# Trunk kernel: V split before the normalising products, k prepared before q, and K's other half written by ScalarE and GpSimd

## The chip, the cores and the metric

The kernel runs on one core of a Trainium2 chip. The metric is the device time of one execution in microseconds (us), the median of several runs. The core has five engines that each work through a list of instructions of their own and wait for one another with semaphores: TensorE (PE in the profile) multiplies matrices and transposes, VectorE (DVE) and ScalarE (ACT) do element-wise work and can read PSUM, the memory into which TensorE writes, GpSimd (POOL) does element-wise work on SBUF, and SyncE (SP) issues the transfers (DMAs).

## The reference

A decoder trunk of two layers on x of shape (1, 512, 1024) in float32. Each layer is an RMS norm, an attention mixer with a residual, another RMS norm, and an MLP with a squared ReLU, 1024 to 4096 and back, with a residual.

- Layer 0: one input projection gives 8 heads A (dilated sliding windows with ALiBi) and 8 heads B (a window of 128, two shared k/v heads, learned sinks). The head size is 64.
- Layer 1: 16 heads C with a causal mask and a forget gate, whose cumulated logs are added to the scores.

In all heads q and k are normalised per head before the scores:

```python
aq = rms_norm(aq.reshape(bsz, seq, N_HEADS_A, HEAD_DIM), a_q_gain)
ak = rms_norm(ak.reshape(bsz, seq, N_HEADS_A, HEAD_DIM), a_k_gain)
s = jnp.einsum("bqhd,bqjhd->bhqj", qb, kg).astype(jnp.float32) * scale
p = jnp.exp(s - m)
num = jnp.einsum("bhqj,bqjhd->bhqd", p.astype(v.dtype), vg)
```

## The kernel before

**Numbers as pairs.** TensorE multiplies rounded operands (float32r). Each operand is therefore held as a rounded part and a remainder, high and low, and a product takes three matmuls: high by high, low by high, high by low. Weights arrive by DMA in `wraw` tiles and are split into `whi` and `wlo`; a pattern names the engines that write the two. Activations are split in the same manner, by `scale_split` (L158) where they are scaled too: ScalarE writes the high part, DVE the remainder.

**Layer 0's beginning.** `start` (L613) loads x and the first weights, multiplies for q and k of the first four heads A into four PSUM banks of the pool pA, and builds the distance tables in between. It then calls `norm_heads` (L243): ScalarE copies the banks to `qk` tiles (L250) and squares them (L254), DVE sums the squares per head (L255), and `rsqrt_small` (L120) takes the inverse roots in a chain of small DVE operations (L130 to L135). Since the norm of the whole token enters too, its inverse root is taken in the same chain; the squares' and the roots' scratch lies in one buffer named `sq`. The loop at L271 multiplies q and k by the roots for each of the four blocks of 128 tokens, the first and third on DVE and the others on GpSimd (`NORM`), and L276 copies the token's root to `rcol`.

Then `v_a(0)` multiplies for V into four pA banks. Its `prep_v` (L310) needs `rcol` and splits each bank, which gives the banks back for `kv_b` (k and v of the heads B), and `kv_b` runs as dense work beside the first attention heads.

**Attention.** `run` (L446) interleaves steps of attention (scores, softmax, transposes of P, values) with dense projections, in a fixed proportion, in the program's text. For each pair of heads `get` calls `prep_q` (L286) and then `prep_k` (L297). Each transposes a 128-column block of `qk` on TensorE into a pB bank (`head_T`, L279) and splits it. Q has for each head one half with the high part and the other half with the remainder over the 128 partitions. K has for each head a tile in which `k[:, 0]` is the high part and `k[:, 1]` the remainder, each of them in both halves of the partitions: `scale_split` fills the half in which the head's transpose lies, and a DMA on SyncE's queue (L306) copies both parts to the other half. There are 13 such pairs, 26 K tiles: 4 pairs of heads A, one for the heads B, 8 of heads C.

**What sets the order.** A planner goes over the program with estimated times and orders each engine's list; an instruction that is earlier in the text goes first where both are ready. `in_order` (L144) fixes an instruction behind the one before it on its engine in the text, while `cnt["start"]` holds. In the attention stages nothing is fixed; in the MLP nearly everything is. Tiles with one `tag` share a number of buffers, `bufs`, and a new one waits until an old one is done with. P3 is the tag of the tables' scratch and of the widest P tile.

Of the kernel before, what the change touches and what calls it, by code (L numbers as in the profile page):

```python
# [9 lines left out]
F32 = mybir.dt.float32  # L10
# [59 lines left out]
def trunk(ctx, tc, x, b_sinks, w_out_even, b_forget, w_out_odd, w_up, w_down, xt, gains, w_in_even, w_in_odd, out):  # L70
# [10 lines left out]
    def bank(tag, name):  # L81
        return ps.tile([P, 512], F32, tag=tag, bufs=BANKS[tag], name=name)
# [61 lines left out]
    def in_order(m):  # L144
        if cnt["start"]:
            tc.keep_in_program_order(m)
# [50 lines left out]
    def layer_attention(li, hT, w_in, w_out, stats=None):  # L197


        with ExitStack() as c2:  # L200
# [42 lines left out]
            def norm_heads(outs, nh, sq_tag="sq", sq_bufs=1 + li, ms=None):  # L243


                w = nh * HD
                qk = [ap.tile([P, 2, 512], F32, tag="qk", bufs=4, name="qk") for _ in range(2)]
                ss = small.tile([P, NT, 8], F32, tag="ss", name="ss")
                for t in range(NT):
                    nc.scalar.copy(qk[t // 2][:, t % 2, :w], outs[t][:, :w])  # L250
                for t in range(NT):
                    q = qk[t // 2][:, t % 2, :w]
                    sq = ap.tile([P, 512], F32, tag=sq_tag, bufs=sq_bufs, name="sq")
                    nc.scalar.activation(sq[:, :w], q, AF.Square)  # L254
                    nc.vector.reduce_sum(ss[:, t, :nh], sq[:, :w].rearrange("p (h d) -> p h d", d=HD), axis=AX.X)  # L255
                if ms is None:
                    v = small.tile([P, NT, 8], F32, tag="ssv", name="ssv")[:, :, :nh]
                    rs = small.tile([P, NT, 8], F32, tag="rs", name="rs")[:, :, :nh]
                    room = None
                else:  # L260
                    room = ap.tile([P, 512], F32, tag=sq_tag, bufs=sq_bufs, name="room")
                    room = [room[:, i * NT * (nh + 1):(i + 1) * NT * (nh + 1)]
                            .rearrange("p (t h) -> p t h", h=nh + 1) for i in range(5)]
                    v, rs = room[:2]
                    nc.vector.tensor_scalar(v[:, :, nh], ms, 1.0 / D, EPS, op0=OP.mult, op1=OP.add)
                    nc.vector.tensor_scalar_mul(ecol, v[:, :, nh], EPS)
                for t in range(NT):
                    nc.vector.tensor_scalar(v[:, t, :nh], ss[:, t, :nh], 1.0 / HD, ecol[:, t:t + 1],
                                            op0=OP.mult, op1=OP.add)
                rsqrt_small(rs, v, room)  # L270
                for t in range(NT):  # L271
                    q = qk[t // 2][:, t % 2, :w].rearrange("p (h d) -> p h d", d=HD)
                    eng = nc.gpsimd if NORM[t] == "g" else nc.vector
                    eng.tensor_mul(q, q, rs[:, t, :nh].unsqueeze(2).to_broadcast([P, nh, HD]))
                if ms is not None:
                    nc.vector.tensor_copy(rcol, rs[:, :, nh])  # L276
                return qk

            def head_T(qk, off):  # L279
# [6 lines left out]
            def prep_q(qk, off):  # L286

                pt = head_T(qk, off)
                q = ap.tile([P, 2, 512], F32R, tag="Q", bufs=2, name="Q")
                for h in range(2):  # L290
                    r = slice(h * HD, (h + 1) * HD)
                    r2 = slice((1 - h) * HD, (2 - h) * HD)
                    nc.scalar.copy(q[r, h], pt[r])
                    nc.vector.tensor_sub(q[r2, h], pt[r], q[r, h].bitcast(F32))
                return q

            def prep_k(qk, off, g):  # L297

                pt = head_T(qk, off)
                ks = []  # L300
                for h in range(2):
                    k = ap.tile([P, 2, 512], F32R, tag="K", bufs=3, name="K")
                    r = slice(h * HD, (h + 1) * HD)
                    r2 = slice((1 - h) * HD, (2 - h) * HD)
                    scale_split(k[r, 0], k[r, 1], pt[r], g[r])
                    nc.sync.dma_start(k[r2].bitcast(F32), k[r].bitcast(F32))  # L306
                    ks.append(k)
                return ks

            def prep_v(outs, off, nh, i):  # L310

                V = vset[i % 2]
                for t in range(NT):
                    src = outs[t][:, off:off + nh * HD].rearrange("p (h d) -> p h d", d=HD)
                    scale_split(V[:, t, :nh, :HD], V[:, t, :nh, HD:], src, rcol[:, t:t + 1])
                return V
# [193 lines left out]

            def v_use(g, i):
                def use(outs):
                    st["v", g] = prep_v(outs, 0, 4, i)
                return use

            def qk_use(key, nh, *sq):
                def use(outs, ms=None):
                    st["qk", key] = norm_heads(outs, nh, *sq, ms=ms)
                return use
# [5 lines left out]
            if li == 0:  # L525
                def qk_a(g):
                    return project([(g * 768, g * 768 + 512)], qk_use(g, 8))

                def v_a(g):
                    return project([(g * 768 + 512, g * 768 + 768)], v_use(g, 0), PAT_START if g == 0 else PAT_ATT)  # L530

                def att_a(g):
                    def get(p_):
                        qk = st["qk", g]
                        return prep_q(qk, p_ * P), prep_k(qk, 256 + p_ * P, gg[:, 0:1])
                    return attend(get, 256, lambda: st["v", g], lambda j: j, "a", 4 * g, 2, 2 * g)

                def kv_b():
                    def use(outs):
                        st["v", 3] = prep_v(outs, P, 2, 1)  # L540
                        st["k", "b"] = norm_heads(outs, 2)
                    return project([(2048, 2304)], use, PAT_START)

                def att_b():
                    def get(p_):
                        if p_ == 0:
                            st["kb"] = prep_k(st["k", "b"], 0, gg[:, 1:2])
                        k = st["kb"][p_ // 2]
                        return prep_q(st["qk", "b"], p_ * P), [k, k]
                    return attend(get, 0, lambda: st["v", 3], lambda j: j // 4, "b", 0, 4, 4)  # L550

                start(ap, hT, w_in, make_tables(ap, dist, lt, lb), [bank("pA", f"pj{t}") for t in range(NT)], qk_use(0, 8))
                all_of(v_a(0))
                run(att_a(0), 32, chain(kv_b(), project([(1536, 2048)], qk_use("b", 8))), 768, LEADS[0])
                run(att_b(), NB, chain(qk_a(1), v_a(1)), 768, LEADS[1])
                run(chain(att_a(1), last_values()), 38, chain(out_part([0, 1, 4, 5], True),
                                                              out_part([6, 7], False), ahead([2, 3])), 1536, LEADS[2])
                last = [2, 3]
            else:
                def qk_c(g):  # L560
                    return project([(g * 768, g * 768 + 512)], qk_use(g, 8))

                def v_c(g):
                    return project([(g * 768 + 512, g * 768 + 768)], v_use(g, g))

                def vf_c():
                    def use(outs):
                        forget(ap, outs)
                        v_use(0, 0)(outs)
                    return project([(512, 768), (3072, 3088)], use, PAT_START)  # L570

                def att_c(g):
                    def get(p_):
                        qk = st["qk", g]
                        return prep_q(qk, p_ * P), prep_k(qk, 256 + p_ * P, gg[:, 2:3])
                    return attend(get, 256, lambda: st["v", g], lambda j: j, "c", 4 * g, 2, 2 * g)

                g = vf_c()
                for _ in range(STATS):
                    next(g)  # L580
                stats()
                all_of(g)
                all_of(qk_c(0))
                for g in range(3):
                    run(att_c(g), 36, chain(qk_c(g + 1), v_c(g + 1)), 768, LEADS[3 + g])
                run(chain(att_c(3), last_values()), 42, chain(out_part([0, 1, 2, 3], True),
                                                              out_part([4, 5], False), ahead([6, 7])), 1536, LEADS[6])
                last = [6, 7]
# [683 lines left out]
```

## Time and profile before

| | |
|---|---|
| runs, median (lowest to highest) | 1165.46 us (1165.13 to 1166.15) |
| the profiled execution: its time | 1166.66 us |
| its span in the trace | 1164.9 us |
| mean granted TensorE clock | 0.997 |
| PE busy | 1145.0 us, 98% |
| DVE busy | 875.5 us, 75% |
| ACT busy | 645.9 us, 55% |
| POOL busy | 200.3 us, 17% |

The attention of layer 0 lies from about 45 to 240 us of the span, its MLP from there to about 570, the attention of layer 1 from there to about 830, and its MLP behind that. A row of the timeline has the start in us, the duration in us, engine, line, operation, what it writes and reads, its shape and how many are merged; in brackets the idle time of the engine before it and what ended that. A row of waits has the engine that waited, its line, what it waited for, and then the sum in us, the number of waits and the longest. In tables of windows each engine's busy time is followed by the granted TensorE clock, the busy share of the DMA engines and GB/s.

### The profile page before, as it was taken

To read this page: it belongs to the slowest core of one execution; us is meant where nothing else is said; L and a number is where in the kernel's file an instruction comes from. 1 tells how busy PE (TensorE), PEld (TensorE's weight loads), DVE (VectorE), ACT (ScalarE), POOL (GpSimd) and SP (SyncE) were. 2 spreads that over 40 slices of the span, in tenths; PEclk is the share of its full clock that TensorE was granted. 3 is DMA by queue.
4 is the path that set the end of the run, shared out by engine and by line. 5 is a ranking of instruction groups with operands and counts; after the bars stand their busy time and mean duration, and the time that the engine had idled before them with its cause. 6 is when DMAs were issued, how large, how long until landed. Compare 5 with 4: busy or idle time off the path is not lost.

```text
span 1164.9 us, 17364 instructions
## 1 busy us (share of the span) xinstructions
PE 1145.0 (98%) x6228; PEld 980.3 (84%) x6228; DVE 875.5 (75%) x1865; ACT 645.9 (55%) x1342; POOL 200.3 (17%) x292
## 2 busy tenths in 40 slices
PE   9899999999999999999999999999999999999998
PEld 7887887888988988988887888888888888888887
DVE  7787899968967847855646877778858759669676
ACT  7365867565545545444335685656756455465452
POOL 0345434200000000000155445342100000000000
PEclk9899999999999999999999999999999999999999
DMA  8423115242332332333443333343430721623403
GB/s 287 129 75 91 37 37 148 71 127 73 102 116 91 91 109 91 93 118 106 149 122 121 106 86 109 95 133 112 164 104 4 234 90 56 197 73 109 148 34 109
DMA packets 94695, 126.57 MB, mean 109 GB/s; under 512 B 5888, under 2 KB 66304, under 8 KB 94608
## 3 DMA queue, kind: packets, MB, share of 16 engines
q1 hardware_dynamic: 93568, 123.29, 34.7%
q10 hardware_dynamic: 1040, 2.16, 0.5%
q8 instruction: 49, 0.80, 0.3%
q14 instruction: 38, 0.31, 0.1%
HBM read 114.39 MB, written 4.23 MB: 102 GB/s over the span
## 4 chain that ended last, share of the span: by engine, by line
PE 84%; DVE 7%; DMA 3%; ACT 3%; issue 2%; POOL 2%; SPq 0%; POOLq 0%; ACTq 0%; DVEq 0%
PE up L165 10%; PE up L168 10%; PE up L169 10%; PE pj L236 4%; PE pj L234 4%; PE pj L235 4%; PE O L398 3%; PE PT L378 2%; PE op L169 2%; PE op L165 2%; PE op L168 2%; PE Y L1032 2%; PE Y L1030 2%; PE Y L1033 2%; PE S L341 2%
## 5 line engine op out<-in xcount | busy, mean ns | idle before, releaser
L165 PE MATMUL up<-xin,whi 128*128 128x512 f32 x512 | 200.5, 392 | 0.0
L169 PE MATMUL up<-xin,whi 128*128 128x512 f32 x512 | 199.3, 389 | 0.0
L168 PE MATMUL up<-xin,wlo 128*128 128x512 f32 x512 | 199.2, 389 | 0.0
L779 ACT CAST whi<-wraw 128x512 fp32r<-128x512 f32 x228 | 139.2, 619 | 105.1 <-PE up L169 47.4
L780 DVE TENSOR_TENSOR wlo<-wraw,whi 128x512 fp32r<-128x512 f32 x228 | 151.6, 685 | 50.9 <-ACT whi L779 50.8
L169 PEld LDWEIGHTS up<-xin,whi 128*128 128x128 f32 x512 | 96.1, 188 | 20.2
L165 PEld LDWEIGHTS up<-xin,whi 128*128 128x128 f32 x512 | 96.1, 188 | 19.8 <-issue 0.2
L168 PEld LDWEIGHTS up<-xin,wlo 128*128 128x128 f32 x512 | 96.2, 188 | 19.6 <-issue 0.2
L358 ACT ACTIVATE P<-P,negm 128x128 f32<-128x128 f32 (+5 forms) x128 | 69.4, 543 | 46.5 <-DVE negm L355 44.6
L153 POOL TENSOR_SCALAR whi<-wraw 128x512 fp32r<-128x512 f32 x88 | 60.1, 684 | 167.3 <-PE pj L236 123.6
L961 ACT ACTIVATE u<-up 128x512 f32<-128x512 f32 x64 | 38.3, 599 | 90.9 <-PE up L169 90.9
L234 PE MATMUL pj<-whi,hn 128*128 128x512 f32 (+2 forms) x256 | 88.7, 347 | 0.0
L236 PE MATMUL pj<-whi,hn 128*128 128x512 f32 (+2 forms) x256 | 86.9, 340 | 0.0
L235 PE MATMUL pj<-wlo,hn 128*128 128x512 f32 (+2 forms) x256 | 86.8, 339 | 0.0
L800 DVE TENSOR_TENSOR t<-u 128x256 f32<-128x256 f32 x56 | 23.1, 423 | 62.9 <-ACT u L1104 61.1
L156 POOL TENSOR_TENSOR wlo<-wraw,whi 128x512 fp32r<-128x512 f32 x48 | 64.0, 1335 | 21.0 <-ACT whi L151 18.6
L366 POOL TENSOR_SCALAR P<-P,rden 128x256 f32<-128x256 f32 (+2 forms) x96 | 48.9, 512 | 81.5 <-DVE rden L361 76.0
L156 DVE TENSOR_TENSOR wlo<-wraw,whi 128x512 fp32r<-128x512 f32 (+1 forms) x71 | 48.2, 685 | 18.5 <-POOL whi L153 15.0
L390 ACT CAST PT<-PT 128x256 fp32r<-128x256 f32 (+3 forms) x128 | 49.1, 403 | 21.5 <-PE PT L378 20.6
L234 PE MATMUL pj<-whi,h 128*128 128x256 f32 (+1 forms) x160 | 55.4, 346 | 4.6 <-DVE v L161 4.1
L355 DVE CUSTOM_DVE_ANT_0 P<-S,bias 128x128 f32<-128x128 f32 (+1 forms) x96 | 45.7, 485 | 17.8 <-PE S L344 11.9
L779 ACT CAST whi<-mraw 128x512 fp32r<-128x512 f32 x64 | 38.8, 619 | 33.1 <-DVE mraw L890 14.4
(241 smaller groups left out, 3092.1 us busy)
## 6 DMA issues: line engine op xcount, KB each, us to landing
wraw<-in_w_up SPq DMA_DIRECT2D x64, 512.0 KB, 4.3
wraw<-in_w_down SPq DMA_DIRECT2D x56, 512.0 KB, 3.8
wraw<-in_w_in_odd SPq DMA_DIRECT2D x22, 512.0 KB, 3.8
wraw<-in_w_in_even SPq DMA_DIRECT2D x17, 512.0 KB, 4.7
mraw<-in_w_down SPq DMA_DIRECT2D x16, 512.0 KB, 4.7
K<-K SPq DMA_DIRECT2D x26, 256.0 KB, 2.9
bias<-csp SPq DMA_DIRECT2D x16, 256.0 KB, 3.3
wraw<-in_w_out_odd SPq DMA_DIRECT2D x8, 512.0 KB, 3.8
```

Of the source, the lines that this page charges most:

```text
L153: nc.gpsimd.tensor_scalar(dst_h, src, 1.0, 1.0, op0=OP.mult, op1=OP.mult)
L156: in_order((nc.gpsimd if lo == "pool" else nc.vector).tensor_sub(dst_l, src, dst_h.bitcast(F32)))
L165: m = nc.tensor.matmul(o, wh, xh, start=start, stop=False, skip_group_check=more)
L168: nc.tensor.matmul(o, wl, xh, start=False, stop=False, skip_group_check=more)
L169: nc.tensor.matmul(o, wh, xl, start=False, stop=stop, skip_group_check=more)
L234: nc.tensor.matmul(o, xh, hi[:, :n], start=k == 0, stop=False)
L235: nc.tensor.matmul(o, xh, lo[:, :n], start=False, stop=False)
L236: nc.tensor.matmul(o, xl, hi[:, :n], start=False, stop=k == DC - 1)
L358: nc.scalar.activation(p[:, :ne], p[:, :ne], AF.Exp, scale=-1.0, bias=negm[:, i:i + 1], accum_out=den[:, i:i + 1])
L390: nc.scalar.copy(dst[:, 0], pt[:, :n])
L779: sca(nc.scalar.copy(dst_h, src))
L780: late.append(lambda: vec(nc.vector.tensor_sub(dst_l, src, dst_h.bitcast(F32))))
```

## The change

- `norm_heads` puts the products with the inverse roots into a function, `normalise`. At the start (where the token's norm comes along) it isn't called at once but stored; `v_use`, after V has been split, calls it. V's split and DVE's products are fixed in this order.
- The squares of this first call lie in two buffers with the tag P3, not in one with the tag `sq`.
- `get` of the heads A and C calls `prep_k` before `prep_q`.
- In `prep_k` the DMA is gone. ScalarE writes the high part of the other half from PSUM with a second activation, and GpSimd copies the remainder.

```diff
@@ norm_heads
-                for t in range(NT):
-                    q = qk[t // 2][:, t % 2, :w].rearrange("p (h d) -> p h d", d=HD)
-                    eng = nc.gpsimd if NORM[t] == "g" else nc.vector
-                    eng.tensor_mul(q, q, rs[:, t, :nh].unsqueeze(2).to_broadcast([P, nh, HD]))
-                if ms is not None:
+                def normalise():
+                    for t in range(NT):
+                        q = qk[t // 2][:, t % 2, :w].rearrange("p (h d) -> p h d", d=HD)
+                        eng = nc.gpsimd if NORM[t] == "g" else nc.vector
+                        m = eng.tensor_mul(q, q, rs[:, t, :nh].unsqueeze(2).to_broadcast([P, nh, HD]))
+                        if eng is nc.vector:
+                            in_order(m)
+
+                if ms is None:
+                    normalise()
+                else:
                     nc.vector.tensor_copy(rcol, rs[:, :, nh])
+                    st["first"] = normalise
                 return qk
@@ prep_k
                     scale_split(k[r, 0], k[r, 1], pt[r], g[r])
-                    nc.sync.dma_start(k[r2].bitcast(F32), k[r].bitcast(F32))
+                    nc.scalar.activation(k[r2, 0], pt[r], AF.Copy, scale=g[r])
+                    nc.gpsimd.tensor_copy(k[r2, 1], k[r, 1].bitcast(F32))
@@ v_use
                 def use(outs):
+                    first = st.pop("first", None)
+                    cnt["start"] = first is not None
                     st["v", g] = prep_v(outs, 0, 4, i)
+                    if first:
+                        first()
+                    cnt["start"] = False
                 return use
@@ att_a; att_c in the same manner
-                        return prep_q(qk, p_ * P), prep_k(qk, 256 + p_ * P, gg[:, 0:1])
+                        k = prep_k(qk, 256 + p_ * P, gg[:, 0:1])
+                        return prep_q(qk, p_ * P), k
@@ layer 0
-                start(ap, hT, w_in, make_tables(ap, dist, lt, lb), [bank("pA", f"pj{t}") for t in range(NT)], qk_use(0, 8))
+                start(ap, hT, w_in, make_tables(ap, dist, lt, lb), [bank("pA", f"pj{t}") for t in range(NT)], qk_use(0, 8, "P3", 2))
```

More of the change, by code (lines that the diff above doesn't have):

```diff
@@ L574, in get @@
                         qk = st["qk", g]
-                        return prep_q(qk, p_ * P), prep_k(qk, 256 + p_ * P, gg[:, 2:3])
+                        k = prep_k(qk, 256 + p_ * P, gg[:, 2:3])
+                        return prep_q(qk, p_ * P), k
                     return attend(get, 256, lambda: st["v", g], lambda j: j, "c", 4 * g, 2, 2 * g)
```

## The prediction

> **What bounds the kernel now.** I read the page first, then who waited for whom, then the windows around the largest wait, then the engines one by one in that stretch. The page:
>
> ```profile
> span 1164.9 us, 17364 instructions
> PE 1145.0 (98%) x6228; PEld 980.3 (84%) x6228; DVE 875.5 (75%) x1865; ACT 645.9 (55%) x1342; POOL 200.3 (17%) x292
> PE 84%; DVE 7%; DMA 3%; ACT 3%; issue 2%; POOL 2%; SPq 0%; POOLq 0%; ACTq 0%; DVEq 0%
> ```
>
> TensorE (PE) is busy 98% of the span and carries 84% of the chain that ended last. The change removes no matmul, so it can only win back time in which PE stands still or runs slowly. PE's waits, with the total, the count and the longest in us:
>
> ```profile
> PE pj L234 <- DVE v L161: 4.1, 2, 3.5
> ...
> PE S L341 <- DMA K<-K: 1.9, 3, 1.1
> PE S L341 <- DVE yf L402: 1.3, 1, 1.3
> PE PT L378 <- DVE negm L355: 1.1, 1, 1.1
> PE qkT L283 <- POOL qk L274: 1.0, 2, 0.5
> ```
>
> The largest is the first: kv_b's matmuls wait for a pj bank until V has been read out of it. The second is the transfer that fills K's other half. PE's list shows where the first lies:
>
> ```profile
> 41.35 0.28 PE L235 MATMUL pj<-wlo,h 128*128 128x256 f32 x1
> 41.47 0.28 PE L236 MATMUL pj<-whi,h 128*128 128x256 f32 x1
> 45.25 0.39 PE L234 MATMUL pj<-whi,h 128*128 128x256 f32 x1 [3.50 <-DVE v L161]
> ```
>
> PE ends v_a(0) at 41.75 and stands until 45.25, 3.50 us; of the 4.1 us in two waits 0.6 are left for the second, for the fourth V tile. (Matmuls of this form start 0.12 us apart: 41.35, 41.47.) The windows (from and to, the width, the busy us of PE, of its weight loads, of DVE, ACT and POOL, then the granted clock) show a second cost:
>
> ```profile
> 42.00:44.00 2.00, 0.00 (x0) 0.00 (x0) 2.00 (x2) 0.00 (x0) 2.00 (x2) 1.00 0.00 0
> ...
> 46.00:48.00 2.00, 1.38 (x8) 0.99 (x7) 1.57 (x2) 0.00 (x0) 0.63 (x1) 0.59 0.00 0
> 48.00:50.00 2.00, 2.00 (x11) 2.00 (x11) 0.08 (x1) 0.58 (x1) 0.00 (x0) 0.50 0.71 223
> 50.00:52.00 2.00, 2.00 (x11) 2.00 (x11) 1.69 (x3) 1.61 (x3) 0.00 (x0) 0.50 0.10 39
> 52.00:54.00 2.00, 2.00 (x15) 2.00 (x14) 0.91 (x2) 0.34 (x1) 0.62 (x1) 0.70 0.61 131
> ...
> 160.00:200.00 40.00, 36.80 (x208) 30.93 (x207) 37.59 (x99) 26.21 (x69) 17.46 (x22) 1.00 0.40 114
> ```
>
> After the standstill the granted clock is 0.59, 0.50, 0.50 and 0.70 in four windows of 2 us, with PE busy nearly all the time: 2 x (0.41 + 0.50 + 0.50 + 0.30) = 3.4 us of matmul time lost. So this place costs 3.50 + 0.6 + 3.4 = 7.5 us.
>
> **Part 1: V before the products with the norms.** Why V comes late is on DVE's list, with ScalarE's and GpSimd's rows beneath it:
>
> ```profile
> 40.81 0.20 DVE L135 SCALAR_TENSOR_TENSOR room<-room 128x36 f32<-128x36 f32 x1
> 41.04 2.14 DVE L274 TENSOR_TENSOR qk<-qk,room 128x512 f32<-128x512 f32 x2
> 43.11 1.00 DVE L276 COPY rcol<-room 128x4 f32<-128x4 f32 x1
> 44.71 1.27 DVE L161 SCALAR_TENSOR_TENSOR v<-pj,rcol,v 128x256 fp32r<-128x256 f32 x3 [0.60 <-ACT v L160]
> 45.90 1.28 DVE L156 TENSOR_TENSOR wlo<-wraw,whi 128x512 fp32r<-128x512 f32 x1
> ```
> ```profile
> 44.21 1.57 ACT L160 ACTIVATE v<-pj,rcol 128x256 fp32r<-128x256 f32 x4 [9.05 <-DVE rcol L276]
> ```
> ```profile
> 41.14 2.95 POOL L274 TENSOR_TENSOR qk<-qk,room 128x512 f32<-128x512 f32 x2 [3.07 <-issue]
> ```
>
> The inverse roots are done at 41.01. Two products (2.14) and the copy of rcol (1.00) stand before V, and ScalarE has been idle 9.05 us for rcol. Moved behind V, these products cost V nothing. rcol then follows the roots at once: 0.17 us by a 128x4 operation alone (quoted below), 1.00 by its own row beside GpSimd's products. I take 0.2, because GpSimd started 0.1 us after DVE in the row above.
>
> **Part 2: squares with two buffers, under P3's name.** ScalarE's squares wait for DVE's reductions, one buffer between them (ScalarE's waits from 28 to 40; its last cast of V's and kv_b's weights; a small DVE operation alone):
>
> ```profile
> ACT sq L254 <- DVE ss L255: 1.2, 3, 0.7
> ```
> ```profile
> 33.67 0.60 ACT L151 CAST whi<-wraw 128x512 fp32r<-128x512 f32 x1
> ```
> ```profile
> 35.91 0.17 DVE L265 TENSOR_SCALAR room<-ms 128x4 f32<-128x4 f32 x1
> ```
>
> The three waits sum to 1.2 us. The gain is between 0 (if the tables' scratch, which has the same name, still holds a buffer) and 1.2; I take 1.2, since those tables are finished before the squares begin. Roots end at 39.8, rcol at 40.0. ScalarE's V tiles start 0.1 later at 0.39 each (1.57 for four), DVE's 0.5 behind them: the first bank is free near 41.1, before PE ends at 41.75. The fourth tile's matmuls end only at 41.75, so it is through near 42.8; PE asks for it after three triples of 3 x 0.12 = 0.36, at 42.8. PE's idle time left here: I take 0.3, between 0 and 1.9 (no gain from the buffers, and the full 1.00 for rcol). **Parts 1 and 2: 3.50 + 0.6 - 0.3 = 3.8, and the clock's 3.4, together 7.2 us.** What is late next is qk: its two DVE products end near 42.8 + 2.14 = 44.9 instead of 43.18. Cover is kv_b: 32 triples at 0.36 are 11.5 us of matmuls that need only V's banks. The last cast of its weights, at 33.67 above, is done by 34.3. Without that cover the whole 3.2 us would be idle again (a rival below).
>
> **Part 3: K's other half by ScalarE and GpSimd.** K's rows (min/median/max ns), and its transfer's landing:
>
> ```profile
> L160 ACT ACTIVATE K<-qkT,gg x26: 682/684/689, 50.2 to 789.6; 64x512 fp32r<-64x512 f32 x26
> L161 DVE SCALAR_TENSOR_TENSOR K<-qkT,gg,K x26: 735/750/757, 50.9 to 790.4; 64x512 fp32r<-64x512 f32 x26
> L306 SPq DMA_DIRECT2D K<-K x26: 461/467/522, 51.7 to 791.2; - x26
> ...
>   ACT K L160: 4.0, 12
> ...
> DMA to landing us min/median/max: 2.8/2.9/4.9
> ```
> ```profile
> L156 POOL TENSOR_TENSOR wlo<-wraw,whi 128x512 fp32r<-128x512 f32 x48 | 64.0, 1335 | 21.0 <-ACT whi L151 18.6
> L153 POOL TENSOR_SCALAR whi<-wraw 128x512 fp32r<-128x512 f32 x88 | 60.1, 684 | 167.3 <-PE pj L236 123.6 <-DVE room L265 22.8 <-issue 7.4
> L366 POOL TENSOR_SCALAR P<-P,rden 128x256 f32<-128x256 f32 x40 | 22.1, 554 | 10.8 <-DVE rden L361 10.4
> ```
>
> Removed: 26 issues on SP and 2.9 us from issue to landing after each DVE part. SP's queue only becomes freer: a weight load no longer stands behind an issue that waits for K. Added: 26 ScalarE activations of the same form as L160, 0.684 each, 17.8 us; and 26 GpSimd copies of 64x512, which no row shows: 0.554 by the 128x256 row, 1.335 by the two-input row. I take 0.684, the row with one input and 512 columns: 17.8 us. After DVE's part K is complete in about 0.7 us, not 2.9, so the 1.9 us of PE's wait for K go: **gain 1.9** (0 to 1.9). k ahead of q delays Q by at most the four K activations, 2.7 us, but S needs both, and K with its transfer was the later one.
>
> What the additions cost others: ScalarE is 3% of the chain, 35 us of its 646 busy, so 5.4% of what it does sets the end: 17.8 x 0.054 = 1.0. GpSimd by the same sum: 23 of 200.3 are 12%, 2.1; I take 0.8, because the copy stands where the transfer's wait was. **Cost 1.8 us**, between 0 and 17.8 (all of ScalarE's addition on the path). DVE may also be slowed by GpSimd's copies: the product with two SBUF inputs at 45.90 took 1.28 beside GpSimd, but K's own L161, which reads PSUM, keeps to 735-757 throughout. I take nothing.
>
> [...]
>
> **Sum.** 7.2 + 1.9 - 1.8 = 7.3 us. The profiled execution took 1166.66 us, 1.76 more than its span; the runs shown have a median of 1165.46, 1.2 below it. 1166.66 - 7.3 = 1159.4 profiled, 1158.2 as a median. The instructions of the attention stages are ordered by a planner and will be ordered anew; PE's waits of 1.3, 1.1 and 1.0 above may grow or vanish: 2.5 us either way. With the other bounds the forecast's own range is 1155.0 to 1161.4.
>
> **Rivals.**
>
> A, *partly given back* in attention. From 160 to 200 DVE is busy 37.59 of 40 us, PE 36.80: there DVE, not PE, may set the pace, and PE's earlier arrival turns into waiting. For it: the waits on negm and yf. Against: DVE's own start is moved ahead too, and it has idle time to spare just behind the stall, 1.92 us of 2 from 48 to 50 and 1.09 of 2 from 52 to 54. Half of 7.2 lost: 1161.8.
>
> B, *the stall changes its name*: if the planner puts the transposes of qk ahead of kv_b's matmuls, PE waits from 41.75 to 44.9 for qk's products, 3.2 us. For it: PE already waits 1.0 for GpSimd's qk later on. Against: kv_b is ready when V is, and qk isn't. If the clock falls as before, 3.50 + 0.6 - 3.2 = 0.9 and 1.9 - 1.8 remain: 1164.5. [...] The trace shows the fall once, after 3.50 us.
>
> C, *slower*: ScalarE's additions come to lie on the path. ScalarE already waits 4.0 us in 12 places for DVE's K part, in order, and the added activation reads the same bank: each pair holds that bank and the running head's exponentials behind it 1.37 us longer. It decides from 9.1 + 2.3 = 11.4 of the 17.8 us, 64%. For it: exponentials feed the P that PE transposes. Against: the 55% busy, and 3% on the chain. At three quarters exposed: 1165.5 - 9.1 + 13.4 = 1169.8.
>
> **How the numbers follow.** Forecast 0.61, A 0.19, B 0.11, C 0.09. About 0.2%, 2.3 us, can be told from no change. The forecast and A are faster, 0.80; B is the same, 0.11; C is slower, 0.09. The range runs from 1154.5, below the forecast's own lower end, to 1164.0, which takes in A and part of B.
>
> **What would show it.** In the changed profile: rcol ahead of the first L274 on DVE; PE's wait for v under 1 us near 41.7; the granted clock at 1.00 from 40 to 60; no wait for K's transfer; 52 activations of K's form on ScalarE, 26 copies on GpSimd near 0.7 us. Wrong if the clock still falls to 0.50 there (B), if PE's waits for ScalarE or P grow by several us between 60 and 240 or 620 and 800 (A, C), or if the copies take over 1.3 us.

## The result, and the profile after

| | before | after |
|---|---|---|
| median of the runs beside each other (lowest to highest) | 1165.51 us (1165.13 to 1166.15) | 1172.40 us (1170.73 to 1174.19) |
| ratio, 95% interval | | 1.0058 (1.0047 to 1.007) |
| the profiled execution: time, span | 1166.66, 1164.9 us | 1174.19, 1172.4 us |

The change makes the kernel 6.9 us slower, 0.58%. The forecast was 1158.2 us. The page of the changed kernel (span, busy time of the engines, chain by engine):

```profile
span 1172.4 us, 17345 instructions
...
PE 1151.0 (98%) x6228; PEld 980.3 (84%) x6228; DVE 875.8 (75%) x1865; ACT 665.7 (57%) x1368; POOL 216.2 (18%) x318
...
PE 83%; DVE 8%; DMA 3%; POOL 2%; ACT 2%; issue 2%; SPq 0%; POOLq 0%; DVEq 0%; ACTq 0%
```

ScalarE and GpSimd are busy 19.8 and 15.9 us longer, as planned, and their shares of the chain are hardly other than before. TensorE runs the same 6228 instructions and shows 6.0 us more busy time. So the page alone names no culprit. The forecast's own signs come out well at the start. The lists of PE, DVE and ScalarE around V:

```profile
44.29 0.39 PE L234 MATMUL pj<-whi,h 128*128 128x256 f32 x1 [0.94 <-DVE v L161]
```
```profile
39.98 0.17 DVE L282 COPY rcol<-room 128x4 f32<-128x4 f32 x1
...
44.16 1.97 DVE L275 TENSOR_TENSOR qk<-qk,room 128x512 f32<-128x512 f32 x2
```
```profile
40.25 1.21 ACT L160 ACTIVATE v<-pj,rcol 128x256 fp32r<-128x256 f32 x3 [5.93 <-DVE rcol L282]
```

rcol now stands ahead of the products and takes 0.17 us, and PE waits 0.94 us for V where it waited 3.50. The windows (columns as before: busy time of PE, its weight loads, DVE, ACT, POOL, then the granted clock) show that the clock's fall at 46 us is gone, and that it has come back elsewhere:

```profile
46.00:48.00 2.00, 2.00 (x20) 2.00 (x19) 0.73 (x2) 1.15 (x2) 0.11 (x1) 1.00 0.43 165
48.00:50.00 2.00, 2.00 (x16) 1.75 (x14) 1.91 (x6) 1.81 (x3) 1.11 (x2) 1.00 0.00 0
...
104.00:106.00 2.00, 1.43 (x6) 0.84 (x7) 1.15 (x2) 0.29 (x1) 1.92 (x3) 0.90 0.00 0
106.00:108.00 2.00, 2.00 (x7) 1.52 (x6) 0.68 (x1) 1.55 (x3) 1.84 (x2) 0.50 0.00 0
108.00:110.00 2.00, 2.00 (x13) 1.90 (x12) 0.89 (x3) 0.47 (x2) 0.18 (x1) 0.74 0.00 0
```

The last three lose 2 x (0.10 + 0.50 + 0.26) = 1.7 us. The same happens once more from 162 to 168, so the clock costs 3.4 us in this execution, as much as before. (Behind TensorE's last matmul the clock falls once more, here to 0.64 in the window from 1170 to 1172 us, in e1_again at 1159.34; that costs nothing and isn't counted here or below.) K's rows and PE's waits after:

```profile
L160 ACT ACTIVATE K<-qkT,gg x26: 682/683/687, 46.7 to 796.0; 64x512 fp32r<-64x512 f32 x26
L161 DVE SCALAR_TENSOR_TENSOR K<-qkT,gg,K x26: 732/750/757, 47.4 to 797.1; 64x512 fp32r<-64x512 f32 x26
L313 ACT ACTIVATE K<-qkT,gg x26: 680/683/687, 48.2 to 798.5; 64x512 fp32r<-64x512 f32 x26
L314 POOL CAST K<-K x26: 604/607/941, 48.6 to 798.2; 64x512 fp32r<-64x512 f32 x26
```
```profile
PE S L349 <- DVE Q L301: 2.3, 5, 0.7
...
PE O L406 <- ACT PT L398: 1.5, 1, 1.5
PE qkT L290 <- DVE qk L275: 1.4, 2, 0.8
PE PT L386 <- DVE yf L410: 1.4, 1, 1.4
PE S L350 <- POOL K L314: 1.3, 1, 1.3
...
PE pj L234 <- DVE v L161: 0.9, 1, 0.9
```

The additions cost what was estimated for each, 0.683 and 0.607 us, and the wait for K's transfer (1.9) is gone. In its place stand many small waits for Q, P, K and the values, none above 1.5 us. Where the time goes is seen from a few matmuls that every trace has. The table gives their times in before (the start of a score, the end of the values), and how far other kernels are ahead (-) or behind (+), read off PE's list in each trace:

| matmul | before, us | after | e1_start | e5_start_kwrite | i1_after_order | i3_dummy_order |
|---|---|---|---|---|---|---|
| first score of layer 0 | 56.38 | -7.4 | -5.2 | -7.4 | -5.0 | -4.7 |
| last values of layer 0 | 217.11 | +2.2 | -6.0 | -1.8 | -4.0 | -3.0 |
| first score of layer 1 | 626.25 | -1.3 | -5.7 | -4.6 | -5.3 | -3.0 |
| last values of layer 1 | 815.10 | +7.1 | -5.8 | +3.1 | -5.2 | -2.3 |
| PE's end | 1161.20 | +7.1 | -5.8 | +3.3 | -5.2 | -2.3 |

By name the changed kernel is 7.4 us ahead at its first score, but part of that is only that its scores stand earlier in TensorE's list. By place in the list (about the 300th matmul, at 59 us in before) it is 4.8 us ahead; it is 2.2 behind from the end of layer 0's attention through the MLP, and 7.1 behind from the end of layer 1's. So 7.0 us are lost in the first attention stage, 3.4 of them to the clock's two falls, 4.9 in the second, and nothing elsewhere. The other columns are experiments.

### The profile page after: what moved, and what is told of

Its sections match the earlier page's. It is cut to its first block, busy times and chain, and to the rows that moved or that the text cites. A ratio compares the mean times of both kernels' runs of the same rounds, so it can differ in the third digit from the quotient of the medians.

```text
span 1172.4 us, 17345 instructions
## 1 busy us (share of the span) xinstructions
PE 1151.0 (98%) x6228; PEld 980.3 (84%) x6228; DVE 875.8 (75%) x1865; ACT 665.7 (57%) x1368; POOL 216.2 (18%) x318
## 4 chain that ended last, share of the span: by engine, by line
PE 83%; DVE 8%; DMA 3%; POOL 2%; ACT 2%; issue 2%; SPq 0%; POOLq 0%; DVEq 0%; ACTq 0%
PE up L165 10%; PE up L169 10%; PE up L168 10%; PE pj L235 4%; PE pj L236 4%; PE pj L234 4%; PE O L406 3%; PE PT L386 2%; PE op L169 2%; PE Y L1047 2%; PE Y L1045 2%; PE Y L1048 2%; PE op L165 2%; PE op L168 2%; PE S L349 2%
## 5 line engine op out<-in xcount | busy, mean ns | idle before, releaser
L794 ACT CAST whi<-wraw 128x512 fp32r<-128x512 f32 x228 | 139.2, 619 | 105.5 <-PE up L169 47.2
L168 PEld LDWEIGHTS up<-xin,wlo 128*128 128x128 f32 x512 | 96.2, 188 | 19.8 <-issue 0.2
L165 PEld LDWEIGHTS up<-xin,whi 128*128 128x128 f32 x512 | 96.1, 188 | 19.8 <-issue 0.2
```

What stands on the lines that cost most here:

```text
L165: m = nc.tensor.matmul(o, wh, xh, start=start, stop=False, skip_group_check=more)
L168: nc.tensor.matmul(o, wl, xh, start=False, stop=False, skip_group_check=more)
L794: sca(nc.scalar.copy(dst_h, src))
```

## The experiments

Differences below are medians against the kernel before on the same chip.

**First: the three parts apart.** e1_start keeps the start's part only (the function `normalise` and the squares in P3), e2_kwrite only the write, e3_korder only k ahead of q, e4_start_korder the start and k ahead of q.

Against the kernel before, e2_kwrite and then e3_korder (its second place, att_c, alike):

```diff
-                    nc.sync.dma_start(k[r2].bitcast(F32), k[r].bitcast(F32))
+                    nc.scalar.activation(k[r2, 0], pt[r], AF.Copy, scale=g[r])
+                    nc.gpsimd.tensor_copy(k[r2, 1], k[r, 1].bitcast(F32))
```
```diff
-                        return prep_q(qk, p_ * P), prep_k(qk, 256 + p_ * P, gg[:, 0:1])
+                        k = prep_k(qk, 256 + p_ * P, gg[:, 0:1])
+                        return prep_q(qk, p_ * P), k
```

> V ahead of the products and the squares in two P3 buffers alone; K is filled by the transfer and q is prepared first, as before. Theory W (the writing of K's other half on ScalarE and GpSimd costs the time): the early gain of 7.4 us, which the changed kernel shows at the first scores, stays: 1158 to 1160 us, layer 1 lasts as long as before. Theory O (k ahead of q costs it): the same, 1158 to 1160. Theory A (attention in layer 0 gives back what arrives early, whatever is done with K): 1164 to 1167, with the first scores about 7 us earlier and layer 0's attention ending where it did, near 217 us.

Measured: 1161.24 us, -4.3, ratio 0.9962 (0.9948 to 0.9975). The lead is 5.8 us at 80 us and stays between 5.6 and 6.0 through both attention stages, so these give nothing back. The time is a little above what W and O gave and well below A's.

> Only K's other half by ScalarE and GpSimd in place of the transfer; the start and q first as before. Theory W: slower by what layer 1 lost in the changed kernel, 4.9 us, and as much or more in layer 0: 1170 to 1178 us. Theory O: about as before, 1164 to 1167, or 1.9 us faster by the waits for the transfer. Theory A: layer 1 slower by 4.9 us, layer 0 unchanged: 1170.

Measured: 1175.58 us, +10.1, ratio 1.0081 (1.0065 to 1.0097).

> Only k ahead of q; the transfer and the start as before. Theory O: slower, layer 1 by 4.9 us and layer 0 by up to 9: 1170 to 1178 us. Theory W: within 1.5 us of before, 1164 to 1167, or faster by some of the 1.9 us that PE waited for the transfer. Theory A: as W.

Measured: 1171.48 us, +6.0, ratio 1.0049 (1.0033 to 1.0065). PE's waits in e3_korder:

```profile
PE S L341 <- DMA K<-K: 7.4, 5, 2.3
PE pj L234 <- DVE v L161: 3.5, 1, 3.5
```

The wait for K's transfer is 7.4 us where it was 1.9, although k is transposed first. K's transfers also take longer from issue to landing:

```profile
DMA to landing us min/median/max: 2.8/3.6/6.0
```

Before had 2.8/2.9/4.9. Of the 26 transfers 11 take more than 4 us here, 4 in before.

> The changed kernel with the transfer put back: V first, two P3 buffers, k ahead of q. Theory W: 1156 to 1160 us, the gain at the start kept, and the transfer's waits shorter since it starts earlier. Theory O: 1168 to 1173, nearly as slow as the changed kernel. Theory A: 1164 to 1167.

Measured: 1167.94 us, +2.4, ratio 1.0026 (1.0016 to 1.0036): 6.7 above e1_start. So the start gains, each of the two other parts loses by itself, and the parts don't add: -4.3 + 10.1 + 6.0 is +11.8, and all together are +6.9.

**Second: which piece of the write.** All four have the start's part and q ahead of k. e5_start_kwrite has the full write; x6_act_hi lets ScalarE write the high part and leaves the remainder to a transfer; x7_pool_lo leaves the high part to a transfer and adds nothing on ScalarE; x8_act_sbuf lets ScalarE copy from K's tile, so that the PSUM bank is not held.

Against e1_start, x6_act_hi, x7_pool_lo and x8_act_sbuf in turn:

```diff
-                    nc.sync.dma_start(k[r2].bitcast(F32), k[r].bitcast(F32))
+                    nc.scalar.activation(k[r2, 0], pt[r], AF.Copy, scale=g[r])
+                    nc.sync.dma_start(k[r2, 1].bitcast(F32), k[r, 1].bitcast(F32))
```
```diff
-                    nc.sync.dma_start(k[r2].bitcast(F32), k[r].bitcast(F32))
+                    nc.sync.dma_start(k[r2, 0].bitcast(F32), k[r, 0].bitcast(F32))
+                    nc.gpsimd.tensor_copy(k[r2, 1], k[r, 1].bitcast(F32))
```
```diff
-                    nc.sync.dma_start(k[r2].bitcast(F32), k[r].bitcast(F32))
+                    nc.scalar.copy(k[r2, 0], k[r, 0].bitcast(F32))
+                    nc.gpsimd.tensor_copy(k[r2, 1], k[r, 1].bitcast(F32))
```

> The start's part and the write by ScalarE and GpSimd, q first: the changed kernel without k ahead of q. If the parts add, 1161.2 + 10.1 = 1171 us by all theories of the write; if the write is only dear where it meets the old start, 1163 to 1166.

Measured: 1170.69 us, +4.7, ratio 1.0042 (1.0027 to 1.0057), with the granted clock at 1.00 throughout.

> The start's part, q first; K's high part in the other half by ScalarE from PSUM, the remainder by the transfer, no GpSimd copy. Theory Q (0.68 us more on ScalarE for each K tile, in order, in front of the exponentials) and theory H (ScalarE's late read keeps the PSUM bank of K's transposes longer): slow, 1167 to 1171. Theory G (GpSimd's copy) and theory P (without a transfer in K's path the planner puts the scores earlier into PE's list than the other engines can serve them): as with the start alone, 1160 to 1163.

Measured: 1170.41 us, +4.4, ratio 1.0041 (1.0026 to 1.0056).

> The start's part, q first; K's high part in the other half by the transfer, the remainder by GpSimd, nothing more on ScalarE. Theories Q, H and P: as with the start alone, 1160 to 1163. Theory G: slow, 1166 to 1171.

Measured: 1174.11 us, +8.1, ratio 1.008 (1.0063 to 1.0097).

> The start's part, q first, and the write by ScalarE and GpSimd, but ScalarE copies the high part from the SBUF tile that it has just written instead of scaling PSUM's once more, so the bank is free when DVE has read it. Theory H: the loss goes, 1161 to 1164. Theories Q and P: as slow as with PSUM, 1169 to 1172.

Measured: 1169.22 us, +3.2, ratio 1.0032 (1.0019 to 1.0045).

All are slow: without any work added on ScalarE (x7), without GpSimd (x6), and without the longer hold of the bank (x8). None of the three can be the sole cause. Theory P fell too in the form that it had: x6 and x7 still have a transfer in K's path and are slow. The clock blurs the comparison: in the profile its falls take 5.1 us in x7 and 3.4 in x8, and nothing in e5 and x6. What the four have in common shows in PE's list. One pair of heads of layer 1 in e1_start's second run and in the changed kernel (start, duration, line, tiles; of the products between the first and the last are shown):

```profile
673.64 0.93 PE L290 MATMUL qkT<-ident,qk 128*128 128x128 f32 x7
674.33 0.48 PE L236 MATMUL pj<-whi,hn 128*128 128x512 f32 x1
...
679.41 0.39 PE L234 MATMUL pj<-whi,hn 128*128 128x512 f32 x1
679.64 0.39 PE L235 MATMUL pj<-wlo,hn 128*128 128x512 f32 x1
679.87 0.28 PE L348 MATMUL S<-K,Q 128*128 128x256 f32 x1
...
681.65 0.48 PE L348 MATMUL S<-K,Q 128*128 128x512 f32 x1
...
683.58 1.09 PE L405 MATMUL O<-PT,v 128*128 128x512 f32 x5
```
```profile
681.19 0.93 PE L290 MATMUL qkT<-ident,qk 128*128 128x128 f32 x7
681.87 0.48 PE L234 MATMUL pj<-whi,hn 128*128 128x512 f32 x1
...
683.80 0.39 PE L236 MATMUL pj<-whi,hn 128*128 128x512 f32 x1
684.32 0.36 PE L349 MATMUL S<-K,Q 128*128 128x256 f32 x1
...
689.01 0.48 PE L349 MATMUL S<-K,Q 128*128 128x512 f32 x1
...
692.70 1.18 PE L406 MATMUL O<-PT,v 128*128 128x512 f32 x5
```

With the transfer the planner puts 24 dense products between the transposes and the first score, which then starts without a wait. Without it only 9 stand there, and the score waits: it starts 0.52 us behind the last product (683.80, 684.32), where above it followed after 0.23 (679.64, 679.87), as one product follows another. The head's four scores take 4.7 us from first to last start instead of 1.8, but that is mostly no loss: the planner has put 12 of the dense products in between. The mean over the eight pairs of layer 1, counted in each list:

| kernel | matmuls between transposes and first score | against before, us |
|---|---|---|
| before; e1_start | 26.4; 26.4 | 0; -4.3 |
| e3_korder; e4_start_korder | 24.0; 24.0 | +6.0; +2.4 |
| x7_pool_lo | 19.1 | +8.1 |
| x6_act_hi; e5_start_kwrite; e2_kwrite | 13.9; 13.6; 13.6 | +4.4; +4.7; +10.1 |
| after | 10.6 | +6.9 |
| x8_act_sbuf | 9.0 | +3.2 |

All six kernels with a changed write have shorter distances than before, but the loss doesn't rise with the shortening, so the count is a sign and no price.

**Third: the list held.** The order of PE's matmuls in e1_start was written down and imposed on other kernels:

```diff
+    pe = [i for i in nc.cur_bb.bb.instructions if "Matm" in type(i).__name__]
+    order = [k for run in PE_ORDER.split() for a, n in [map(int, run.split("+"))] for k in range(a, a + n)]
+    for a, b in zip(order, order[1:]):
+        tc.add_manual_dep(pe[b], pe[a].name,
+                          mybir.DependencyInfo(mybir.DependencyClass.NoSync, mybir.DependencyReason.DATA),
+                          reason="order")
```

f1_dummy leaves the list to the planner and adds the work alone, into a tile `kd` that nothing reads; h1_order holds the list under the write. f1_dummy against e1_start:

```diff
+                    kd = ap.tile([P, 512], BF16, tag="Kd", bufs=1, name="Kd")
+                    nc.scalar.activation(kd[r2], pt[r], AF.Copy, scale=g[r])
+                    nc.gpsimd.tensor_copy(kd[r2], k[r, 1].bitcast(F32))
```

> The start's change as in e1_start, K's other half still by the transfer, q ahead of k; beside it every K tile gets one more ScalarE activation of K's form and one more GpSimd copy, both into a tile that nothing reads. The added work is extra and is no part of the result. TensorE's list has the same order as in e1_start (26.4 matmuls on the mean between the last transpose and the first score of a pair). Occupancy (the added instructions on ScalarE and GpSimd and the longer hold of the PSUM bank cost the 9 us by themselves): 1168 to 1171. Order (the planner's new order of TensorE's list costs them): 1161 to 1163, within 0.2% of e1_start.

Measured: 1165.51 us, -0.1, ratio 0.9997 (0.9988 to 1.0006): 4.2 worse than e1_start and 4.8 better than e5_start_kwrite, so it fits neither theory. Its list was not e1_start's in layer 0 after all, only in the count for layer 1, and the clock fell twice (103 and 625 us, 3.4 us together). It is repeated below with the list held.

> The start's change, and K's other half written by ScalarE and GpSimd (as in e5_start_kwrite), but TensorE's matmuls are held in the order of e1_start's list, matmul for matmul. Order: 1158 to 1162, since the scores have their 26.4 matmuls of cover again and the transfer's wait of 1.9 us is gone. Occupancy: 1168 to 1171, as e5_start_kwrite.

Measured: 1162.58 us, -3.1, ratio 0.9977 (0.9967 to 0.9986), just above the range of the theory of the order. The same work as e5_start_kwrite in another order is 7.8 us faster, and in neither profile does the clock fall while TensorE works. TensorE's list isn't the only one that is other: the planner orders the remaining engines' lists around the held one, and at least 237 of DVE's 1865 instructions, 192 of ScalarE's 1368 and 49 of GpSimd's 318 stand in another place than in e5_start_kwrite. So the run tells what the planner's new order costs, not what TensorE's list costs alone.

> The whole change, with TensorE's matmuls held in e1_start's order (k's transposes stand in q's places and q's in k's). Order: the loss is in the list, so 1160 to 1163. If k ahead of q costs its 6 us in some other way than by the list: 1166 to 1169. If neither the list nor that order explains the loss: about 1172 as after.

Measured: 1162.46 us, -2.5, ratio 0.9981 (0.9972 to 0.9989). The whole change, with all of its additions, is faster than before once the list is held, and 9.4 us faster than with the planner's list. Its page and its waits:

```profile
PE 1143.0 (98%) x6228; PEld 978.8 (84%) x6228; DVE 873.8 (75%) x1865; ACT 661.2 (57%) x1368; POOL 214.4 (18%) x318
```
```profile
PE S L372 <- DVE yf L433: 2.4, 2, 1.2
...
PE S L372 <- DVE Q L324: 1.3, 1, 1.3
```

PE shows 8.0 us less busy time than in the changed kernel, for the same instructions, of which 3.4 are the clock's (its two falls there; here it doesn't fall before the last matmul). Its idle time is 17.6 us instead of 21.4. So "busy" holds a good part of the loss.

What that is can be counted from the starts of the matmuls. From each interval between neighbouring starts in the two attention stages the usual (median) interval for that pair of forms is taken off, and the clock's falls are left out. What is left is late starts:

| late in sum, us | all | scores | transposes | values | dense products |
|---|---|---|---|---|---|
| e5_start_kwrite against h1_order | 7.9 | 3.5 | 3.3 | 1.1 | 0.0 |
| after against i1_after_order | 8.0 | 5.5 | 1.2 | 1.0 | 0.3 |

The dense products run as before. The matmuls that need another engine's result start late, mostly by 0.1 to 1 us each. For after the 8.0 and the clock's 3.4 make up nearly all of the 11.8 us between the two spans.

> f1_dummy (the start's change, K by the transfer, and one more ScalarE activation and GpSimd copy per K tile that nothing reads; the added work is no part of the result), with TensorE's matmuls held in e1_start's order. If the additions cost nothing by themselves: 1161 to 1162.5. If f1_dummy's 4.3 us were the additions' own and not its new list: 1164.5 to 1166.

Measured: 1164.15 us, -0.8, ratio 0.9991 (0.9983 to 1.0), and 3.2 above e1_again on the same chip, between the two outcomes and just below the second. The additions have a cost of their own. Where it lies is uneven: in the profile 0.9 us is lost near 106, 1.1 between 165 and 194, 1.2 between 630 and 650, and nothing over the last six pairs of layer 1. (Another 0.8 us is lost by 41 us, ahead of the first K tile, and so not to the additions.)

> The start's change and k ahead of q, K's other half by the transfer (e4_start_korder), with TensorE's matmuls held in e1_start's order as in i1_after_order. Order: within 1.5 us of e1_start, 1160 to 1163, and TensorE's waits for K's transfer back from 6.0 to below 2 us. If K's transfers themselves come at a worse time with k first: 1166 to 1168 as e4_start_korder.

Measured: 1165.67 us, +0.8, ratio 1.0002 (0.9993 to 1.001): 4.7 above e1_again, so holding the list takes little of k's cost back, and the theory of the order fails for this part where the transfer stays. In the profile the kernel is 6.5 us behind e1_again: 3.4 are the clock, which fell at 104 and at 626 us, the rest waits (for K's transfer 2.9 instead of 1.4, for yf 2.2 instead of 1.2). Of the 26 transfers 9 still take more than 4 us to land. With the write by ScalarE and GpSimd k ahead of q costs next to nothing: i1_after_order has it and h1_order hasn't, -2.5 and -3.1, which is within the noise.

> The same kernel as e1_start, beside the other three on one chip: 1160.5 to 1162, and no slower than any of the three.

Measured: 1160.99 us, -3.9, ratio 0.9968 (0.9955 to 0.998). It is the fastest version here, ahead of the kernel before and of the changed one.

**Fourth: controls of the holding.** Both kernels are held in e5_start_kwrite's own list.

> e5_start_kwrite (the start's change and the write by ScalarE and GpSimd, q ahead of k), with TensorE's matmuls held in the order that its own list has anyway. If the order is what costs: 1169 to 1172, as e5_start_kwrite. If holding a list by hand is itself a gain: 1161 to 1166.

Measured: 1171.39 us, +5.8, ratio 1.0052 (1.0037 to 1.0067). Holding a list is no gain by itself; which order it is decides. (The other engines' lists are those of e5_start_kwrite here too.)

> e1_start (the start's change alone, K's other half by the transfer), with TensorE's matmuls held in e5_start_kwrite's order: nothing is added on ScalarE or GpSimd. If the order costs by itself: 1170 or more, and beyond it up to 2.9 us a pair where a score now stands ahead of its transfer's landing. If the order costs only together with the additions: 1161 to 1164.

Measured: 1212.82 us, +47.2, ratio 1.041 (1.0392 to 1.0427). Its largest wait:

```profile
PE S L368 <- DMA K<-K: 29.0, 11, 3.7
```

In this list a score stands ahead of its transfer's landing, and the clock falls ten times: TensorE is busy for 35.0 us at half speed, which loses 17.5. Of 50.3 us of span above e1_again 27.6 are that wait and 17.5 the clock. Some 5 us remain for the order itself, so the run says little on that, and a good deal on what a distance of 26 matmuls does: with it the waits for the transfer sum to 1.4 us (e1_again), where in this list, with 13.6, they sum to 29.0.

**Fifth: the start's part split.** e9_norm_only has only the products behind V, e10_sq_only only the buffers of the squares.

The second, against the kernel before (the first is e1_start with this line put back):

```diff
-                start(ap, hT, w_in, make_tables(ap, dist, lt, lb), [bank("pA", f"pj{t}") for t in range(NT)], qk_use(0, 8))
+                start(ap, hT, w_in, make_tables(ap, dist, lt, lb), [bank("pA", f"pj{t}") for t in range(NT)], qk_use(0, 8, "P3", 2))
```

> Of the start only the products with the norms behind V; the squares keep their one buffer; K by the transfer, q ahead of k. By the prediction's terms it keeps the gain but for the 1.2 us that the buffers bring to the roots: the wait for V is then about 1.5 to 1.9 us rather than 0.9. If such a gap still brings the clock down: 1164 to 1165; if not: 1161.5 to 1163.

Measured: 1163.73 us, -1.9, ratio 0.9988 (0.9978 to 0.9998). The wait for V is 1.7 us and the clock stays at 1.00 in the profile, 4.1 us ahead at PE's end; the median lies between the two outcomes.

> Of the start only the squares with two buffers; the products with the norms stay ahead of V. The roots come 1.2 us earlier, so TensorE's gap shrinks from 3.5 to about 2.3 us. If the clock still falls: 1164 to 1165; if a gap of 2.3 us does not bring it down: 1160.5 to 1162.

Measured: 1164.43 us, -1.2, ratio 0.9991 (0.9981 to 1.0). The waits for V are 2.7 us with 1.8 the longest. The clock stays at 1.00 there and falls at 105.4 us instead, which loses 1.7 us. Either half alone brings 1 to 2 us, both 4.

## Why the prediction was wrong, point by point

- **The step that failed** is "The instructions of the attention stages are ordered by a planner and will be ordered anew; PE's waits of 1.3, 1.1 and 1.0 above may grow or vanish: 2.5 us either way." It was 9.4 us one way (after against i1_after_order), 7.8 without k ahead of q (e5_start_kwrite against h1_order), and 8.9 by the control. The forecast took 2.9 us of transfer out of K's path and kept the rest of the list where it was. But without the transfer the planner moves the scores ahead by some 13 matmuls. That cover had cost nothing, and without it scores, transposes and values start late in small pieces, about 8 us in sum. The new order as a whole is shown to be the cause; how much of it is TensorE's list and how much the other engines' lists, which changed with it, stays open. That the planner's estimate of K is what moves the scores is inferred: the distance follows what fills K (26.4 by transfer, 19.1 and 13.9 with one half of it by transfer, 13.6 and 9.0 without), and extra work that K doesn't depend on leaves it at 26.4. Why x6_act_hi's transfer keeps so little of the distance isn't known.
- **Part 3's own sum** was 1.9 gained and 1.8 lost. DVE's busy time is as before (875.8 and 875.5 us), so GpSimd's copies held none of it back that shows. With the list held the write and k's order together cost 1.5 us (i1_after_order against e1_again). The additions alone cost 3.2 (i3_dummy_order), not 1.8, and the difference, 1.7, is near the 1.9 expected of the transfer's wait. The mis-sized term is GpSimd's: the shares of the chain gave 1.0 + 2.1 = 3.1, and the 2.1 was cut to 0.8 because the copy stands where the transfer's wait was. That 3.1 meets the measured 3.2 is luck at least in part: the shares are averages over the span, and the cost lay in a few places.
- **k ahead of q** was costed at nothing, since S needs both. That holds with the write (0.6 us), not with the transfer: +6.0 in e3_korder. There the transfers themselves land later. The pair that is issued at 620.6 us, 0.66 us behind a transfer of weights, lands after 4.7 and 4.5 us; in before it is issued 1.49 us behind that transfer and lands after 3.4 and 3.0. Holding TensorE's list leaves that nearly as it is (9 of 26 above 4 us in i2_korder_order), which fits its loss. That the nearness to the weights is the reason isn't shown.
- **Parts 1 and 2** had the right mechanism: rcol first, no fall of the clock near 46 us, a wait for V under 1 us. The size was 5.8 us in the profile, not 7.2: the wait is 0.9 instead of 0.3, and qk isn't quite covered by kv_b: its transposes waited 1.2 us for DVE's products instead of 0.6. Besides, 0.3 of the 7.2 was counted twice, since TensorE stood for 0.6 us of the 6.83 us at half speed. The medians gain 4.3 and 3.9 only, because the 1.2 us between before's profiled execution and its median was carried over to the changed kernel. e1_start's executions have no such distance: 1160.85 profiled, 1161.24 median.
- **Rival A** (half given back in attention) falls: the start's lead is the same at 80 us and at the end. Of **rival B**'s 3.2 us, 0.6 came true, the wait for qk above. **Rival C** had the sign but not the reason: x7_pool_lo, without an added activation, is slow (by 3 us even without the clock's 5.1), and i1_after_order, with all 26, is faster than before.
- Together: 1158.2 + 2.9 (the start: 1161.1 by e1's two medians) + 1.6 (part 3: 1.5 lost instead of 0.1 gained) + 9.4 (the list) is 1172.1; measured were 1172.4.

## What to carry to other kernels

Where a planner orders an engine's list, a shorter latency is an input to the planner before it is a gain: count the matmuls between producer and consumer in the old list, and ask whether a list that is made for the shorter latency still has that cover. To judge such a change, hold the old order under the new work once: here that turned +6.9 us into -2.5 and separated the planner's order from the additions. Look at the other engines' lists as well, since they follow the held one. And a profiled execution's distance from its median belongs to that kernel alone.

## What the runs showed of the hardware

The clock fell without a long standstill too, and not every time. In before it fell after a wait of 3.50 us, in i2_korder_order after three of 0.51 to 0.65 us; after the same three it didn't in e1_again. PE's list and windows (PE alone, then clock, DMA share, GB/s) of e1_again and of i2_korder_order in the same stretch:

```profile
100.83 0.30 PE L290 MATMUL qkT<-ident,qk 128*128 128x128 f32 x1 [0.65 <-DVE qk L275]
101.64 0.33 PE L290 MATMUL qkT<-ident,qk 128*128 128x128 f32 x1 [0.51 <-POOL qk L275]
103.09 0.33 PE L290 MATMUL qkT<-ident,qk 128*128 128x128 f32 x1 [0.54 <-POOL qk L275]
```
```profile
101.00 0.30 PE L313 MATMUL qkT<-ident,qk 128*128 128x128 f32 x1 [0.65 <-DVE qk L298]
101.81 0.33 PE L313 MATMUL qkT<-ident,qk 128*128 128x128 f32 x1 [0.51 <-POOL qk L298]
103.26 0.33 PE L313 MATMUL qkT<-ident,qk 128*128 128x128 f32 x1 [0.55 <-POOL qk L298]
```
```profile
97.79:101.21 3.42, 2.69 (x12) 1.00 0.79 220
101.21:104.62 3.41, 2.43 (x11) 1.00 0.40 87
```
```profile
96.90:100.32 3.42, 3.42 (x16) 1.00 0.47 102
100.32:103.73 3.41, 1.71 (x9) 1.00 0.76 205
103.73:107.14 3.41, 3.41 (x12) 0.50 0.00 0
```

After the same waits the clock stays at 1.00 in one kernel and is at 0.50 in the other. In a trace with several falls these lie a whole number of 3.413 us apart (in i2_korder_order 103.73 and 625.97, 153 times; in after 105.61 and 163.64, 17 times), and each one during the work lasts 3.41 us (both in after) or twice that (6.83 in before); one of 3.41 us loses 1.7 us where TensorE is busy. The windows above are laid in steps of that length, in i2_korder_order so that one ends at the fall at 103.73, in e1_again back from its fall behind the last matmul (1159.34 us). So laid, i2_korder_order has the waits in one window, in which TensorE is busy for 1.71 of 3.41 us, and e1_again has them in two, with 2.69 and 2.43. In the 3.41 us before a fall during the work TensorE was busy for 1.10 us in before, for 1.50 and 1.86 in after and for at least 1.9 in x7_pool_lo (the fall at 107.4), while a window with 1.6 brought none in e10_sq_only (40.5 to 43.9, laid back from its fall). So the busy time of a window goes with the falls only roughly, and the traces give no sharp limit. The same three small waits were followed by a loss of 1.7 us in one kernel and by none in the other; what decides between the two isn't shown.
